# Experts of a two-layer trunk taken in an order that the chip decides, with weights addressed by loaded ids

## The chip, the cores and the metric

One core of one Trainium2 chip runs the whole program. The metric is device time in microseconds for one execution; lower is better. Engines are called PE (matmul), PEld (weight load of PE), DVE, ACT, POOL and SP, as in the profile. All weight transfers are issued by SP.

## What is computed

The input is 256 frames of 1024 float32 values. There are two layers. Each has a norm, an input projection with three token mixers, an output projection, and a second norm. Then layer 0 has a dense SwiGLU, and layer 1 the part that this change touches, the top-2-of-8 expert SwiGLU:

```
logits = t @ router                      # 256 tokens, 8 experts
top_v, top_i = lax.top_k(logits, 2)
gates = one_hot(top_i) * softmax(top_v)
for e in range(8):
    out = out + gates[:, e:e+1] * (silu(t @ wg[e]) * (t @ wu[e])) @ wd[e]
```

Each expert has three matrices of 1024 x 3584 float32, so 3 x 1024 x 3584 x 4 bytes = 44.04 MB, and eight experts have 352.3 MB. Every expert's weights are read whole, however many of the 256 tokens chose it. On average 64 tokens choose an expert (256 x 2 / 8). A final norm follows.

## The kernel before

**The weight stream.** A `Stream` (L72 to L134) holds a list of pieces of at most 1 MB, in the order in which PE will need them: the weights of the layers, then expert 0, 1, ..., 7. `loads` (L104) issues a piece as soon as a slot of the ring is free, by `load` (L156), which makes one transfer on SP's queue for each part of a slot (L162). `done` (L129) is called when the matmuls of a unit are through, and gives its slot back. There are 14 slots of 1 MB. `Room.take` (L783) adds four more, each of two halves of 0.5 MB, once the layers' working buffers are free. These 18 slots are all that the transfers can run ahead of PE.

**An expert.** Each expert is worked through in 7 chunks (NEC) of 512 columns. A chunk has 4.19 MB for the gate and up products and 2.10 MB for the down product, 6.29 MB in all. `experts` (L804) runs over e and c: the gate and up products of chunk c (`up_first`, L863), then `swish`, then the down product of the chunk before (`down`, L910), then three transposes that turn the new activations (`turn`, L891, the PE instructions of L894). With c = 1 the result of the expert before is put back into the rows of x (`combine`, L939). From c = 2 on, the tokens of the next expert are gathered, a step per chunk (`gather`, L823).

**Two sizes of expert.** The first 64 tokens of an expert go through matmuls of 64 columns (`wide`, L848, instructions of L852). If an expert has more than 64, up to 32 further tokens go through extra matmuls of 32 columns (`slim`, L855, instructions of L860), which read the same weights again. `count` (L758) sums the chosen tokens and makes the flag `many` per expert; `reach` (L811) loads it into a register of PE and `extra` (L815) branches on it. A third case (over 96 tokens, L1116 on) repeats the experts, and this input does not reach it. In the text that follows, an expert with the extra matmuls is called heavy, one without light.

**Expert 0's opening.** `opening` (L1074) works the gate product of expert 0's first chunk for all 256 tokens, and between its matmuls runs the router (`choose`, `places`, `counted`). Then `room.take()`, then the rest of `gather(0)`, then the loop. `weighing` (L1108) makes the gates in steps that lie behind the chunks of expert 0.

The order of the work on every engine is the order of the program (`manual_schedule`, L150): an instruction that waits holds up all that stands behind it on its engine.

Of the kernel before, what the change touches and what calls it, by code (L numbers as in the profile page):

```python
# [10 lines left out]
F32 = mybir.dt.float32  # L11
F32R = mybir.dt.float32r
I32 = mybir.dt.int32
AF = mybir.ActivationFunctionType
ALU = mybir.AluOpType
AX = mybir.AxisListType

P = 128
D = 1024
S = 256  # L20
NT = 2
# [10 lines left out]
E = 8  # L32
DFE = 3584
NEC = DFE // 512
EPS = 1e-6
QW = 1024
# [5 lines left out]
RAW = 2048  # L42
NRAW = 14
HALF = 64
# [27 lines left out]
class Stream:  # L72


    def __init__(self, load, split, chunks, slots):


        self.load, self.split = load, split
        self.pieces, self.units = [], []
        for ap, sizes, *more in chunks:  # L80
            whole = more[0] if more else False
            per = more[1] if len(more) > 1 else max(1, RAW // max(sizes))
            at = 0
            for j in range(0, len(sizes), per):
                group = sizes[j:j + per]
                off = 0
                for n in group:
                    self.units.append((len(self.pieces), off, n, off + n == sum(group), whole))
                    off += n
                b, at0 = (ap, at) if len(ap.shape) == 2 else (ap[at // RAW], at % RAW)  # L90
                self.pieces.append(b[:, at0:at0 + off])
                at += off
        self.tiles, self.parts, self.slots = {}, {}, deque(slots)
        self.loaded = self.cut = self.used = self.freed = 0
# [9 lines left out]
    def loads(self, upto=None):  # L104
        while self.slots and self.loaded < min(len(self.pieces) if upto is None else upto, len(self.pieces)):
            self.tiles[self.loaded] = self.slots.popleft()
            self.load(self.tiles[self.loaded], self.pieces[self.loaded])
            self.loaded += 1

    def release(self, i):  # L110
# [27 lines left out]
def trunk_kernel(ctx, tc, x_in, w_in, w_out, ffn_gu, ffn_d, moe_gu, moe_d, router,  # L138
                 params, gains, gm_gain, gm_wsT, pool_w, conv_pw, consts, pool_m, out):
    nc = tc.nc  # L140
# [10 lines left out]
    V, A, G, T = nc.vector, nc.scalar, nc.gpsimd, nc.tensor  # L151
# [31 lines left out]
    for l in range(DEPTH):  # L183
        col = 0
        for _, width in GROUPS:
            n = QW // width * width
# [5 lines left out]
        if l == 0:  # L192
            for c in range(NFC + 1):
                if c < NFC:
                    chunks.append((ffn_gu[c], [QW] * 4))
                if c:
                    chunks.append((ffn_d[c - 1], [QW] * 2))

    def expert_chunks(opening):
        ch = []  # L200
        last = E * NEC
        for i in range(last + 1):
            per = 1 if i >= last - 1 else 2
            if i < last:
                ch.append((moe_gu[i // NEC, i % NEC], *(([QW] * 8, True, per) if i or not opening else ([RAW] * 4, gates, 1))))
            if i:
                ch.append((moe_d[(i - 1) // NEC, (i - 1) % NEC], [QW] * 3 + [512] * 2 if i == last else [QW] * 4,
                           True, per))
        return ch

# [7 lines left out]
    iota1 = cst[:, CC_IOTA:CC_IOTA + P]  # L218
# [15 lines left out]
    gate = con.tile([P, NT, E], F32, name="gate")  # L234
    pos = con.tile([P, NT, E], F32, name="pos")
# [475 lines left out]
    lt = cst[:, CC_LT:CC_LT + E * E].rearrange("p (a b) -> p a b", a=E)  # L711
# [34 lines left out]
    def weigh_a(t, L, sv, vs):  # L746
        V.tensor_tensor(out=sv[:], in0=sel[:, t, :], in1=L[:], op=ALU.mult)
        V.tensor_reduce(out=vs[:], in_=sv[:], axis=AX.X, op=ALU.add)
        V.tensor_scalar(out=vs[:], in0=vs[:], scalar1=-0.5, scalar2=None, op0=ALU.mult)

    def weigh_b(t, L, sv, vs):
        A.activation(sv[:], L[:], AF.Tanh, bias=vs[:])

    def weigh_c(t, sv):
        V.tensor_scalar(out=sv[:], in0=sv[:], scalar1=0.5, scalar2=0.5, op0=ALU.mult, op1=ALU.add)
        V.tensor_tensor(out=gate[:, t, :], in0=sv[:], in1=sel[:, t, :], op=ALU.mult)

    def count(mo):  # L758

        ps = acc.tile([P, 512], F32, tag="acc", name="ps_n")  # L760
        for t in range(NT):
            T.matmul(ps[:, :E], ones, sel[:, t, :], start=(t == 0), stop=(t == NT - 1))
        many = mo.tile([P, E], I32, name="many")
        V.tensor_scalar(out=many[:], in0=ps[:, :E], scalar1=HALF + 0.5, scalar2=None, op0=ALU.is_gt)
        most = mo.tile([P, 1], F32, name="most")
        V.tensor_reduce(out=most[:], in_=ps[:, :E], axis=AX.X, op=ALU.max)
        mosti = mo.tile([P, 1], I32, name="mosti")
        V.tensor_copy(mosti[:], most[:])
        return many, mosti


    class Room:


        def __init__(self, mo):
            self.Sg = [mo.tile([P, NT, P], F32, name="Sg%d" % i) for i in range(2)]
            self.ST = [mo.tile([P, NT, P], F32R, name="ST%d" % i) for i in range(2)]
            self.s = mo.tile([P, 3, P], F32, name="silu2")
            self.ah = [mo.tile([P, 3, P], F32, name="eah%d" % i) for i in range(2)]
            self.yl = mo.tile([P, 512], F32R, name="yl")  # L780
            self.ys = None
# [22 lines left out]
    def experts(room, tok, W, gf, weighing=(), opening=None, counts=None):  # L804
# [3 lines left out]
        weighing = list(weighing)  # L808
# [6 lines left out]
        def extra(e, do):  # L815

            if counts:
                with tc.If(index[e] > 0):  # L818
                    do()
            else:  # L820
                do()
# [26 lines left out]
        def wide(ps, at, left, right, start, stop):  # L848

            for r in range(2):  # L850
                w = right(r)
                T.matmul(ps[HALF * r:HALF * (r + 1), at:at + w.shape[-1]], left, w,  # L852
                         start=start, stop=stop, skip_group_check=True)
# [25 lines left out]
        def flat(s):  # L879
            return s[:, :2, :].rearrange("p a b -> p (a b)")  # L880
# [71 lines left out]
        held, opened = opening(coming) if opening else (None, None)  # L952
        room.take()
        list(coming)
        pend, late = None, 0
        for e in range(E):
            coming = gather(e + 1) if e + 1 < E else iter(())
            for c in range(NEC):
                have = opened and e + c == 0
                if have:  # L960
                    us = held
                    for t in range(NT):
                        wide(room.gu, 0, room.Sg[0][:, t, FIRST], lambda r: opened[t][:, 256 * r:256 * (r + 1)],
                             t == 0, False)
                    for t in range(NT):
                        slim(room.gx, 0, room.Sg[0][:, t, LAST], lambda r: opened[t][:, P * r:P * (r + 1)],
                             t == 0, False)
                    up_first(e, us, True)
                    up_last(e, us, True)
                    A.activation(flat(room.s), room.gu[:, :256], AF.Copy)  # L970
                    A.activation(room.s[:, 2, :], room.gx[:, :P], AF.Copy)
                else:
                    W.pump(12)
                    us = [W.get() for _ in range(KD)]
                    up_first(e, us)
                    extra(e, lambda: up_last(e, us))
                for _ in range(4 if have else KD):
                    W.done()
                if c == 1:
                    if e == 0:  # L980
                        turn(room.ah[0])
                    else:
                        for hf in range(2):
                            combine(e - 1, hf, *late[hf])
                swish(have)
                if pend:
                    us = [W.get() for _ in range(4)]
                    down(*pend, us)
                    for _ in range(4):
                        W.done()  # L990
                    if pend[1] == NEC - 1:
                        late = [cut_y(hf) for hf in range(2)]
                    turn(room.ah[c % 2])
                if c > 1:
                    next(coming, None)
                if e == 0 and 1 < c < 2 + len(weighing):
                    weighing[c - 2]()
                pend = (e, c, room.ah[c % 2])
        e, c, ah = pend
        W.pump(5)  # L1000
# [45 lines left out]
    products, ps = mixing(0, mx, hh, hl, lambda: put(1, hs1))  # L1046
# [3 lines left out]
    with tc.tile_pool(name="ff", bufs=2) as ff:  # L1050
        g = gain(1)
        products, ps = ffn(ff, hh, hl, lambda: put(1, hs1), g)
# [9 lines left out]
    products, ps = mixing(1, mx, hh, hl, lambda: put(1, hs1))  # L1062
    mix_ctx.__exit__(None, None, None)
    mo = ctx.enter_context(tc.tile_pool(name="mo", bufs=1))
# [4 lines left out]
    Ls, counts = [None] * NT, []  # L1069
# [37 lines left out]

    def weighing():  # L1108
        sv = [(mo.tile([P, E], F32, name="sv%d" % t), mo.tile([P, 1], F32, name="vs%d" % t)) for t in range(NT)]
        return [lambda: [weigh_a(t, Ls[t], *sv[t]) for t in range(NT)],  # L1110
                lambda: [weigh_b(t, Ls[t], *sv[t]) for t in range(NT)],
                lambda: [weigh_c(t, sv[t][0]) for t in range(NT)]]

    room = Room(mo)
    experts(room, tok, W, gf, weighing(), opening, counts)
# [100 lines left out]
```

## Time and profile before

| | |
|---|---|
| median of 3 runs | 1272.27 us (1272.19 to 1273.04) |
| profiled execution | 1270.93 us |
| its span, first to last instruction | 1269.1 us |
| PE busy | 1176.0 us, 93% |
| DVE busy | 368.3 us, 29% |
| read from memory | 416.92 MB, 329 GB/s over the span |

The span is what the trace shows; the profiled execution's own time is 1.8 us longer, and the median of the runs is 1.3 us above that. A busy share of 93% for PE is an average over stages; the rate of the transfers, slice by slice, shows where PE waits for weights and where the transfers wait for room.

### The profile page before, as it was taken

What the parts mean: (1) busy time and instruction counts of PE and PEld (TensorE: products, weight loads), DVE (VectorE), ACT (ScalarE), POOL (GpSimd) and SP (SyncE); (2) the same over time, 40 slices, a digit from 0 to 9 for tenths busy, and PEclk for the clock granted to TensorE, in tenths of its full rate; (3) what the DMA queues carried; (4) which work ended last, traced back from release to release, by engine and by line L of the source; (5) the groups of instructions that cost most, each with busy time, mean ns of one, the idle gap of its engine ahead of it and who ended that gap; (6) DMA issues with size and microseconds to landing.
All of it is one profiled execution on the core that took longest, in us unless ns stands there. A gap on an engine that the chain in (4) does not pass through costs nothing. (4 is left out here: it accounts for less than half of the span.)

```text
span 1269.1 us, 17754 instructions
## 1 busy us (share of the span) xinstructions
PE 1176.0 (93%) x7278; PEld 611.7 (48%) x7278; DVE 368.3 (29%) x727; ACT 264.7 (21%) x555; POOL 78.9 (6%) x77
## 2 busy tenths in 40 slices
PE   6999999999999999999999999999999988888882
PEld 5867888889776333343334343433333322322220
DVE  5966455557962111100200020002112111002003
ACT  4545444445541001000100010001001010001001
POOL 2720000003700000000000000000000000000000
PEclk9999999999999999999999999999999999999996
DMA  9945555455346999999989899899999999999991
GB/s 369 425 158 183 196 171 196 136 196 204 125 149 237 418 424 423 423 426 404 370 356 364 350 373 340 335 382 404 424 423 424 424 423 423 424 425 423 422 401 50
DMA packets 72762, 419.72 MB, mean 331 GB/s; under 512 B 8768, under 2 KB 9280, under 8 KB 33856
## 3 DMA queue, kind: packets, MB, share of 16 engines
q1 hardware_dynamic: 72496, 417.77, 82.5%
q8 instruction: 88, 1.44, 0.4%
q10 hardware_dynamic: 144, 0.23, 0.1%
q14 instruction: 34, 0.28, 0.1%
HBM read 416.92 MB, written 1.05 MB: 329 GB/s over the span
## 5 line engine op out<-in xcount | busy, mean ns | idle before, releaser
L852 PE MATMUL ps_gu<-wraw,hh 128*64 128x512 f32 (+1 forms) x1504 | 338.0, 594 | 16.5 <-DMA wraw<-in_moe_gu_dram 15.8
L852 PEld LDWEIGHTS ps_gu<-wraw,hh 128*64 128x64 f32 x1504 | 102.4, 137 | 222.9 <-issue 170.4
L852 PE MATMUL ps_y<-wraw,eah 128*64 128x512 f32 x592 | 137.4, 599 | 11.4 <-DMA wraw<-in_moe_wd_dram 5.1
L167 ACT ACTIVATE whi<-wraw 128x1024 fp32r<-128x1024 f32 (+1 forms) x106 | 108.2, 1027 | 113.9 <-PE ps_gu L245 65.4
L168 DVE TENSOR_TENSOR wlo<-wraw,whi 128x1024 fp32r<-128x1024 f32 (+1 forms) x83 | 101.1, 1218 | 93.6 <-ACT whi L167 93.2
L886 DVE TENSOR_TENSOR silu<-silu,ps_gu 128x256 f32<-128x256 f32 x56 | 23.5, 419 | 339.3 <-ACT silu L885 334.1
L885 ACT ACTIVATE silu<-ps_gu 128x256 f32<-128x256 f32 x55 | 21.1, 384 | 364.2 <-PE ps_gu L852 364.2
L896 DVE COPY eah<-ps_tp 128x256 f32<-128x256 f32 x56 | 23.8, 424 | 226.5 <-ACT eah L895 226.3
L852 PEld LDWEIGHTS ps_y<-wraw,eah 128*64 128x64 f32 x592 | 41.3, 136 | 98.6 <-issue 72.7
L243 PE MATMUL ps_gu<-whi,hh 128*128 128x512 f32 x192 | 77.6, 404 | 1.1 <-ACT hh L239 0.8
L244 PE MATMUL ps_gu<-wlo,hh 128*128 128x512 f32 x192 | 76.1, 396 | 0.8 <-DVE wlo L168 0.8
L245 PE MATMUL ps_gu<-whi,hl 128*128 128x512 f32 x192 | 76.1, 396 | 0.0
L256 POOL TENSOR_TENSOR ss<-ss,mh 128x1 f32<-128x1 f32 x10 | 5.5, 551 | 1117.9 <-DVE ss L255 1117.9
L852 PE MATMUL ps_y<-wmore,eah 128*64 128x512 f32 x304 | 70.2, 599 | 3.0 <-PEq L818 2.5
L895 ACT ACTIVATE eah<-ps_tp 128x128 f32<-128x128 f32 x56 | 15.5, 278 | 255.9 <-PE ps_tp L894 255.7
L852 PE MATMUL ps_gu<-wmore,hh 128*64 128x512 f32 x288 | 66.9, 600 | 1.3 <-DMA wmore<-in_moe_gu_dram 1.0
L860 PE MATMUL ps_gx<-wraw,hh 128*32 128x256 f32 (+1 forms) x1184 | 66.6, 374 | 0.0
L390 DVE SCALAR_TENSOR_TENSOR ps_conv<-cb,par,ps_conv 128x256 f32<-128x256 f32 x150 | 62.7, 481 | 0.9
L860 PEld LDWEIGHTS ps_gx<-wraw,hh 128*32 128x32 f32 x1184 | 36.6, 110 | 33.4 <-issue 11.7
L168 POOL TENSOR_TENSOR wlo<-wraw,whi 128x768 fp32r<-128x768 f32 (+1 forms) x23 | 48.9, 2138 | 50.3 <-ACT whi L167 36.1
L852 PEld LDWEIGHTS ps_y<-wmore,eah 128*64 128x64 f32 x304 | 21.4, 136 | 46.9 <-issue 40.1
L243 PEld LDWEIGHTS ps_gu<-whi,hh 128*128 128x128 f32 x192 | 36.1, 188 | 10.1 <-ACT hh L239 1.7
(205 smaller groups left out, 1294.8 us busy)
## 6 DMA issues: line engine op xcount, KB each, us to landing
wraw<-in_moe_gu_dram SPq DMA_DIRECT2D x184, 1024.0 KB, 12.7
wraw<-in_moe_wd_dram SPq DMA_DIRECT2D x72, 1024.0 KB, 14.1
wmore<-in_moe_wd_dram SPq DMA_DIRECT2D x76, 512.0 KB, 14.7
wmore<-in_moe_gu_dram SPq DMA_DIRECT2D x72, 512.0 KB, 10.3
wraw<-in_ffn_gu_dram SPq DMA_DIRECT2D x22, 1024.0 KB, 4.9
wraw<-in_ffn_d_dram SPq DMA_DIRECT2D x11, 1024.0 KB, 4.9
wraw<-in_w_out_dram SPq DMA_DIRECT2D x8, 1024.0 KB, 7.2
wraw<-in_w_in_dram SPq DMA_DIRECT2D x6, 1024.0 KB, 4.9
```

What stands on the lines that cost most here:

```text
L167: A.activation(hi[:, :n], src, AF.Copy)
L168: (G if pool else V).tensor_tensor(out=lo[:, :n], in0=src, in1=hi[:, :n], op=ALU.subtract)
L243: T.matmul(ps, xh, wh, start=start, stop=False)
L244: T.matmul(ps, xh, wl, start=False, stop=False)
L245: T.matmul(ps, xl, wh, start=False, stop=stop)
L390: V.scalar_tensor_tensor(out=o, in0=i, scalar=wcol, in1=part[:] if k == n else sums[c], op0=ALU.mult, op1=ALU.add)
L852: T.matmul(ps[HALF * r:HALF * (r + 1), at:at + w.shape[-1]], left, w, start=start, stop=stop, skip_group_check=True)
L860: T.matmul(ps[QUARTER * r:QUARTER * (r + 1), at:at + n], left, w, start=start, stop=stop, skip_group_check=True)
L885: A.activation(flat(s), room.gu[:, :256], AF.Silu)
L886: V.tensor_tensor(out=flat(s), in0=flat(s), in1=room.gu[:, 256:], op=ALU.mult)
L895: A.activation(ah[:, :1, :], tp[:, :1, :], AF.Copy)
L896: V.tensor_copy(ah[:, 1:, :], tp[:, 1:3, :])
```

## The change

After the counts are known, DVE ranks experts 1 to 7 by their count. The positions 1 to 7 of the loop then take the experts in the order heaviest, lightest, second heaviest, second lightest, and so on. Expert 0 stays first. `arrange` builds a 7 x 7 matrix that says which expert goes to which position, and with `permute` brings the counts, the flags, the places of the tokens (`pos`) and later the gates into the new order. The expert's number for each position is loaded into a register of SP (`nc.sync.value_load`, seven of them), and the piece of weights is addressed by that register when its transfer is issued (`bass.ds(ids[p], 1)`). Nothing else of an expert's work changes.

```diff
@@ Stream.__init__
+                if callable(ap):
+                    self.pieces.append(lambda ap=ap, at=at, off=off: ap(at // RAW, at % RAW, off))
+                else:
+                    b, at0 = (ap, at) if len(ap.shape) == 2 else (ap[at // RAW], at % RAW)
+                    self.pieces.append(b[:, at0:at0 + off])
@@ Stream.loads
-            self.load(self.tiles[self.loaded], self.pieces[self.loaded])
+            piece = self.pieces[self.loaded]
+            self.load(self.tiles[self.loaded], piece() if callable(piece) else piece)
@@ expert_chunks
+    ids = {}
+    def of(w, p, c):
+        if p == 0:
+            return w[0, c]
+        return lambda i, at, n: w[bass.ds(ids[p], 1), c, i][:, :, at:at + n].rearrange("a p n -> p (a n)")
...
-                ch.append((moe_gu[i // NEC, i % NEC], *(([QW] * 8, True, per) ...
+                ch.append((of(moe_gu, i // NEC, i % NEC), *(([QW] * 8, True, per) ...
-                ch.append((moe_d[(i - 1) // NEC, (i - 1) % NEC], ...
+                ch.append((of(moe_d, (i - 1) // NEC, (i - 1) % NEC), ...
@@ count
-        V.tensor_scalar(out=many[:], in0=ps[:, :E], scalar1=HALF + 0.5, scalar2=None, op0=ALU.is_gt)
+        n = mo.tile([P, E], F32, name="counts")
+        V.tensor_copy(n[:], ps[:, :E])
+        V.tensor_scalar(out=many[:, :1], in0=n[:, :1], scalar1=HALF + 0.5, scalar2=None, op0=ALU.is_gt)
@@ new
+    def permute(tab, turns):
+        by, tmp = turns
+        V.tensor_tensor(out=tmp[:], in0=by[:], in1=tab.unsqueeze(1).broadcast_to([P, E - 1, E - 1]), op=ALU.mult)
+        V.tensor_reduce(out=tab, in_=tmp[:], axis=AX.X, op=ALU.add)
+    def arrange(mo, many, n):
+        m = E - 1
+        La = n[:, 1:].unsqueeze(2).broadcast_to([P, m, m])
+        Lb = n[:, 1:].unsqueeze(1).broadcast_to([P, m, m])
+        ...
+        V.tensor_tensor(out=tmp[:], in0=Lb, in1=La, op=ALU.is_equal)
+        V.tensor_tensor(out=by[:], in0=Lb, in1=La, op=ALU.is_gt)
+        V.tensor_tensor(out=tmp[:], in0=tmp[:], in1=lt[:, 1:, 1:], op=ALU.mult)
+        V.tensor_tensor(out=by[:], in0=by[:], in1=tmp[:], op=ALU.add)
+        ...
+        V.tensor_reduce(out=rank, in_=by[:], axis=AX.X, op=ALU.add)
+        V.tensor_scalar(out=up, in0=rank, scalar1=2.0, scalar2=1.0, op0=ALU.mult, op1=ALU.add)
+        V.tensor_scalar(out=down, in0=rank, scalar1=-2.0, scalar2=float(2 * m), op0=ALU.mult, op1=ALU.add)
+        V.tensor_tensor(out=up, in0=up, in1=down, op=ALU.min)
+        V.tensor_tensor(out=by[:], in0=iota1[:, :m]..., in1=up..., op=ALU.is_equal)
+        turns = by, tmp
+        V.tensor_copy(rank, iota1[:, :m])
+        permute(rank, turns)
+        V.tensor_copy(idi[:], rank)
+        permute(n[:, 1:], turns)
+        V.tensor_scalar(out=many[:, 1:], in0=n[:, 1:], scalar1=HALF + 0.5, scalar2=None, op0=ALU.is_gt)
+        for t in range(NT):
+            permute(pos[:, t, 1:], turns)
+        for p in range(1, E):
+            ids[p] = nc.sync.value_load(idi[0:1, p - 1:p], min_val=1, max_val=m)
+        return turns
@@ experts
         room.take()
         list(coming)
+        turns = arrange(room.mo, *counts[::2]) if opening else None
@@ weighing: a fourth step, behind chunk 5 of expert 0
+                lambda turns: [permute(gate[:, t, 1:], turns) for t in range(NT)]]
```

## Rows read from the trace of the kernel before

**Rows 1.** Page, part 2: PE's clock, transfer rate, 40 slices of 31.7 us.

```profile
PEclk9999999999999999999999999999999999999996
GB/s 369 425 158 183 196 171 196 136 196 204 125 149 237 418 424 423 423 426 404 370 356 364 350 373 340 335 382 404 424 423 424 424 423 423 424 425 423 422 401 50
```

**Rows 2.** Windows, all engines: length, busy by engine, PE clock, DMA share, GB/s.

```profile
494.20:617.70 123.50, 122.27 (x1071) 50.61 (x1071) 15.30 (x35) 10.27 (x29) 0.00 (x0) 1.00 1.00 415
617.70:741.20 123.50, 122.29 (x1075) 50.59 (x1071) 14.72 (x34) 10.27 (x29) 0.00 (x0) 1.00 0.91 354
741.20:861.50 120.30, 118.79 (x1011) 48.83 (x1007) 14.62 (x34) 10.16 (x29) 0.00 (x0) 1.00 0.92 360
...
861.50:950.90 89.40, 84.95 (x404) 31.61 (x401) 13.94 (x34) 9.50 (x29) 0.00 (x0) 1.00 1.01 422
861.50:1028.20 166.70, 158.59 (x752) 59.23 (x748) 26.61 (x64) 18.18 (x55) 0.00 (x0) 1.00 1.01 422
...
950.90:1042.60 91.70, 85.51 (x400) 31.04 (x400) 13.85 (x35) 9.51 (x29) 0.00 (x0) 1.00 1.01 424
1042.60:1147.40 104.80, 89.30 (x400) 29.16 (x401) 14.17 (x35) 9.51 (x29) 0.00 (x0) 1.00 1.01 424
1147.40:1236.70 89.30, 76.48 (x314) 21.24 (x314) 11.74 (x27) 7.58 (x23) 0.00 (x0) 0.98 1.01 417
```

**Rows 3.** Windows of L860 alone, the extra matmuls: PE and PEld busy.

```profile
494.20:617.70 123.50, 39.09 (x672) 20.40 (x672) 1.00 1.00 415
...
741.20:861.50 120.30, 35.50 (x612) 18.43 (x608) 1.00 0.92 360
...
861.50:950.90 89.40, 0.09 (x4) 0.00 (x0) 1.00 1.01 422
```

**Rows 4.** Waits of SP's queue, 618 to 861 us: total, times, longest.

```profile
SPq L162 <- PE ps_gx L860: 125.7, 49, 11.0
```

**Rows 5.** Waits of SP's queue, 1028 to 1237 us.

```profile
SPq L162 <- DMA wraw<-in_moe_gu_dram: 94.9, 50, 2.9
```

**Rows 6.** Timeline of DVE around the opening: start, duration, instruction, idle before.

```profile
386.97 0.22 DVE L732 TENSOR_TENSOR gt<-gt,eq 128x64 f32<-128x64 f32 x1
387.23 0.22 DVE L734 TENSOR_REDUCE rank<-gt 128x8 f32<-128x64 f32 x1
...
392.74 0.47 DVE L827 TENSOR_SCALAR Sg<-cst,pos 128x128 f32<-128x128 f32 x2
...
397.40 0.42 DVE L839 COPY hh<-ps_tp 128x256 f32<-128x256 f32 x1 [1.30 <-ACT hh L838]
403.02 0.42 DVE L886 TENSOR_TENSOR silu<-silu,ps_gu 128x256 f32<-128x256 f32 x1 [5.20 <-ACT silu L970]
```

**Rows 7.** Timeline of PE in the same stretch.

```profile
393.07 3.87 PE L836 MATMUL ps_tp<-Sg,tok 128*128 128x128 f32 x32 [0.71 <-DVE Sg L827]
...
411.61 0.52 PE L894 MATMUL ps_tp<-cst,silu 128*128 128x128 f32 x3 [0.16 <-PEq L818]
```

**Rows 8.** Timeline of SP's queue in the same stretch: weight transfers issued.

```profile
403.19 0.80 SPq L162 DMA_DIRECT2D wraw<-in_moe_gu_dram  x2
...
411.59 1.75 SPq L162 DMA_DIRECT2D wraw<-in_moe_gu_dram  x4
```

**Rows 9.** Line L1116, a register loaded from a tile: duration ns min/median/max.

```profile
L1116 SPq TENSOR_LOAD <-mosti x1: 750/750/750, 1259.7 to 1259.7; - x1
L1116 SPq FUSED_REGOPS  x1: 191/191/191, 1260.5 to 1260.5; - x1
```

**Rows 10.** Line L162, issues of expert weights on SP: duration ns min/median/max.

```profile
L162 SPq DMA_DIRECT2D wraw<-in_moe_gu_dram x192: 327/328/1543, 278.2 to 1220.7; - x192
L162 SPq DMA_DIRECT2D wraw<-in_moe_wd_dram x77: 327/328/1532, 330.4 to 1231.8; - x77
L162 SPq DMA_DIRECT2D wmore<-in_moe_wd_dram x76: 327/328/1169, 387.2 to 1228.1; - x76
L162 SPq DMA_DIRECT2D wmore<-in_moe_gu_dram x72: 327/328/692, 390.2 to 1200.4; - x72
```

More of the change, by code (lines that the diff above doesn't have):

```diff
@@ L89, in __init__ @@
                     off += n
-                b, at0 = (ap, at) if len(ap.shape) == 2 else (ap[at // RAW], at % RAW)
-                self.pieces.append(b[:, at0:at0 + off])
+                if callable(ap):
[3 more added lines that the diff above has]
+                    self.pieces.append(b[:, at0:at0 + off])
                 at += off
@@ L204, in expert_chunks @@
             if i < last:
-                ch.append((moe_gu[i // NEC, i % NEC], *(([QW] * 8, True, per) if i or not opening else ([RAW] * 4, gates, 1))))
+                ch.append((of(moe_gu, i // NEC, i % NEC), *(([QW] * 8, True, per) if i or not opening else ([RAW] * 4, gates, 1))))
             if i:
-                ch.append((moe_d[(i - 1) // NEC, (i - 1) % NEC], [QW] * 3 + [512] * 2 if i == last else [QW] * 4,
+                ch.append((of(moe_d, (i - 1) // NEC, (i - 1) % NEC), [QW] * 3 + [512] * 2 if i == last else [QW] * 4,
                            True, per))
@@ L768, in count @@
         V.tensor_copy(mosti[:], most[:])
-        return many, mosti
+        return many, mosti, n
+    def permute(tab, turns):
[6 more added lines that the diff above has]
+        Lb = n[:, 1:].unsqueeze(1).broadcast_to([P, m, m])
+        by = mo.tile([P, m, m], F32, name="by")
+        tmp = mo.tile([P, m, m], F32, name="by2")
+        V.tensor_tensor(out=tmp[:], in0=Lb, in1=La, op=ALU.is_equal)
+        V.tensor_tensor(out=by[:], in0=Lb, in1=La, op=ALU.is_gt)
+        V.tensor_tensor(out=tmp[:], in0=tmp[:], in1=lt[:, 1:, 1:], op=ALU.mult)
+        V.tensor_tensor(out=by[:], in0=by[:], in1=tmp[:], op=ALU.add)
+        turn = mo.tile([P, 3, m], F32, name="turn")
+        rank, up, down = (turn[:, i, :] for i in range(3))
+        V.tensor_reduce(out=rank, in_=by[:], axis=AX.X, op=ALU.add)
+        V.tensor_scalar(out=up, in0=rank, scalar1=2.0, scalar2=1.0, op0=ALU.mult, op1=ALU.add)
+        V.tensor_scalar(out=down, in0=rank, scalar1=-2.0, scalar2=float(2 * m), op0=ALU.mult, op1=ALU.add)
+        V.tensor_tensor(out=up, in0=up, in1=down, op=ALU.min)
+        V.tensor_tensor(out=by[:], in0=iota1[:, :m].unsqueeze(2).broadcast_to([P, m, m]),
+                        in1=up.unsqueeze(1).broadcast_to([P, m, m]), op=ALU.is_equal)
+        turns = by, tmp
+        V.tensor_copy(rank, iota1[:, :m])
+        permute(rank, turns)
+        idi = mo.tile([P, m], I32, name="idi")
+        V.tensor_copy(idi[:], rank)
[6 more added lines that the diff above has]
+        return turns
     class Room:
         def __init__(self, mo):
+            self.mo = mo
             self.Sg = [mo.tile([P, NT, P], F32, name="Sg%d" % i) for i in range(2)]
@@ L996, in experts @@
                 if e == 0 and 1 < c < 2 + len(weighing):
-                    weighing[c - 2]()
+                    weighing[c - 2](turns)
                 pend = (e, c, room.ah[c % 2])
@@ L1109, in weighing @@
         sv = [(mo.tile([P, E], F32, name="sv%d" % t), mo.tile([P, 1], F32, name="vs%d" % t)) for t in range(NT)]
-        return [lambda: [weigh_a(t, Ls[t], *sv[t]) for t in range(NT)],
-                lambda: [weigh_b(t, Ls[t], *sv[t]) for t in range(NT)],
-                lambda: [weigh_c(t, sv[t][0]) for t in range(NT)]]
+        return [lambda turns: [weigh_a(t, Ls[t], *sv[t]) for t in range(NT)],
+                lambda turns: [weigh_b(t, Ls[t], *sv[t]) for t in range(NT)],
+                lambda turns: [weigh_c(t, sv[t][0]) for t in range(NT)],
+                lambda turns: [permute(gate[:, t, 1:], turns) for t in range(NT)]]
     room = Room(mo)
```

## The prediction

> **What bounds the kernel now.** I read the forty slices first. After slice 13 the transfers run at about 424 GB/s, then fall to 335 to 404 for ten slices, then return to 424 to the end [rows 1]. PE's clock is full throughout, so the dip is not the clock's. Second, windows cut at the L894 transposes of each expert's first chunk: the seven experts after expert 0, the last one up to the transposes of its last chunk [rows 2]. Third, the same windows for the extra matmuls alone [rows 3]. The three stretches with extra matmuls (the second reads like the first) are those of experts 1, 2 and 3; after 861 us there are none. So experts 1, 2, 3 are heavy and 0, 4, 5, 6, 7 light.
>
> A heavy expert takes 123.5 us and PE is busy for 122.3 of them: PE is the bound. SP's queue waits there for PE's matmuls to give slots back [rows 4]: the ring is full and the transfers idle, at 354 and 360 GB/s. A light expert takes PE 89.4 us where the ring still has stock, which is so up to 1028.2 [rows 2]; the next take longer, up to 104.8 us. That is the transfers' own pace: 44.04 MB at 424 GB/s are 103.9 us. SP waits there for earlier transfers to land [rows 5]. So three slow experts in a row fill the ring and leave the transfers idle, and four quick ones in a row then empty it and leave PE idle.
>
> How much does the ring hold? What PE still has to read, less what still arrives, is the stock. After 494.2 us 296.6 MB arrive (51.3, 43.7, 43.3, 37.7, 38.9, 44.4 and 37.2, each row's length times its rate). PE has then used eight gate-and-up and seven down parts, 48.2 of 352.3 MB, and needs 304.1: the stock is 7.5 MB. By the same sum it is 13.7 MB at 861.5, after the heavy experts: full (172.0 needed, 158.3 still to come). At 1042.6 it is 2.2 MB: empty (83.9 and 81.7). A full ring therefore carries 11.5 MB of surplus.
>
> **The change, part by part.**
>
> The order. Ranks by count put the three heavy experts at ranks 0, 1, 2 of seven, and the positions from 1 on take ranks 0, 6, 1, 5, 2, 4, 3. With expert 0 the run of experts is light, heavy, light, heavy, light, heavy, light, light. PE's work is the same. If it never waits for weights, the time from 494.2 us to the last expert's transposes is the three heavy stretches as they are (367.3 us), two light ones of 89.4, and the 166.7 of the 13 chunks after a full ring [rows 2]: 712.8 us. Now it is 742.5 (the sum of the seven windows). The difference is 29.7 us.
>
> Does PE never wait? One heavy expert brings 123.5 x 0.424 = 52.4 MB and uses 44.04: +8.3. One light expert brings 37.9: -6.1. From 7.5 the first heavy one fills the ring to 13.7; a light one leaves 7.6, far above 2.2; the next heavy one fills it again. After the third heavy one the ring is full and two light ones end the run: that is the stretch 861.5 to 1028.2 over again, which PE went through in 166.7 us at its own pace, and after it only the last down part is left. From the transfers' side: 296.6 MB at 424 GB/s take 699.5 us; with a full ring the first heavy expert loses as now, 123.5 x 9/424 = 2.6 us, and the two others 2.2 MB or 5 us each. That is 712.2, against PE's 712.8. The two bounds meet within a microsecond, so little is left to gain beyond this, and any loss on the transfers' side soon shows.
>
> A figure of the Trainium skill speaks against it. The transfers ran at 422 to 424 GB/s over 375 us and more [rows 2]. The Trainium skill's page "DMA: Bandwidth & Descriptors", section Specifications, gives a limit of memory per core of about 358 GB/s. By that figure 44.04 MB would need an estimated 123 us, a heavy expert's time, and the order would be worth nothing; the trace disagrees wherever the ring has room.
>
> `arrange` on DVE: 20 small operations on 7 x 7 or fewer elements. Dependent operations on 64 elements start 0.26 us apart [rows 6], so 20 x 0.26 = 5.2 us. They begin when the last copy of `gather(0)` ends, 397.8 us, and DVE then has nothing to do until 403.0. Its result of 403.0 is wanted by the transposes of 411.6 [rows 7]. So the cost is nothing; without that cover the whole 5.2 us would stand on PE's path.
>
> The extra copy of the counts stands ahead of the selection matrix `Sg` (392.7), and PE waited 0.71 us for that [rows 6, 7]. It adds one dependent step: +0.3 us. The wait for the flags by PE's register loads comes chunks later. The gates' fourth step has two operations for each half of the tokens, under a microsecond or so on DVE, which idles most of each chunk: nothing.
>
> The seven register loads stand in SP's queue and wait for the ids, the 13th operation of `arrange`: 397.8 + 13 x 0.26 = 401.2 us. Behind them stand all further transfers. One load took SP 0.75 us with 0.19 of arithmetic behind it [rows 9]. Seven in a row are 6.6 us, to 407.8, where the next issue stood at 403.2 [rows 8]. From below it is nothing, if loads overlap; from above 4.6 us of idle transfers, or 2.0 MB. I take the upper value. It comes out of the stock: 7.5 becomes 5.5 MB at 494.2, still above empty, and the first heavy expert makes up 8.3. So it costs PE nothing. It would begin to cost at 5.3 MB, 12 us of hold-up.
>
> Each transfer of experts 1 to 7 gets its address from a register. No row shows such an issue. From below: as now, 0.33 us [rows 10]. From above: the whole sequence of a register load each time, 0.33 + 0.94 = 1.27 us. There are 417 issues for 352.3 MB [rows 10], so 351 after 494.2 us, one in 2.0 us. At either end SP keeps up (446 us of 713), and the transfers in flight cover it. I take a value near the lower end, since the arithmetic of one register took 0.19 us [rows 9], and put its cost at nothing.
>
> Sum against the profiled execution: 1270.9 - 29.7 + 0.3 = 1241.5 us. The median of the runs stands 1.3 us above that execution: 1242.8 us.
>
> **Rivals.**
>
> Slower transfers. If transfers addressed by register move less per second (fewer in flight, or a pause at each), the transfers' side becomes the bound. At 410 GB/s 296.6 MB take 723.4 us, the ring is never full, and the time is 1242.8 + 10.6 = 1253 us. At 400 it is 741.5 and the gain is gone. For it: the bounds meet within a microsecond. Against it: sizes, rows and queue stay the same. Chance 0.11.
>
> SP becomes the bound, the rival on the slower side. Each issue would have to take over 742.5 / 351 = 2.1 us, by address arithmetic, a check of bounds, or a drain at each. At 2.3 us the stretch takes 807 us and the kernel 1337. For it: the operation is in no row, and everything of the stream stands behind it in one queue. Against it: the upper bound from rows is 1.27. Chance 0.08.
>
> No change. Either the order on the chip isn't the one that I read (heavy experts still side by side), or the low rate of the heavy stretches is memory's limit and not a full ring: 354 to 360 GB/s [rows 2] is also what 44.04 MB in 123.5 us come to, 357. Then the transfers would not fill the ring in a heavy expert between light ones. Against the second: SP waits for PE there. About 1272 us. Chance 0.07, of which the memory limit has 0.02.
>
> **How the numbers follow.** The forecast has 0.74, with a range of its own of 1238 to 1248: PE may wait a little in the last two experts, where a full ring just lasts (1 MB less of it is 2.4 us), or wait less in the tail. The whole range is 1237 to 1256; it takes in most of the slower transfers and leaves out SP as the bound and no change. A difference of 0.2% (2.5 us) is about what a measurement of this kernel can tell from none. Faster by more: 0.74 + 0.11 = 0.85. The no-change case gives 0.07 within 0.2%, and SP as the bound 0.08 slower.
>
> **What would show it.** Right: the extra matmuls of L860 come in three stretches of some 120 us with a light expert of some 90 us after each; the rate stays over 410 GB/s but for a short dip at the end of each heavy expert; no window of a light expert takes over 93 us before the last two; SP's waits for the extra matmuls shrink from 126 us in two heavy experts [rows 4] to some 10 us in all three. DVE's block ends before the product of L886 is wanted at 411.6. Wrong: light experts of 100 us or more with 424 GB/s or less and SP waiting on landings (slower transfers), SP's issues of L162 at over 2 us each (SP as the bound), or the flags and extra matmuls side by side as before.

## The result, and the profile after

The changed kernel takes 1239.8 us (median of 4 runs, 1238.7 to 1240.7) against 1272.7 us: a ratio of 0.974, interval 0.9724 to 0.9755. The forecast was 1242.8 us in a range of 1237 to 1256. The profiled execution took 1240.74 us, its span 1239.0.

The page after, part 2, as in [rows 1]:

```profile
PEclk9999999999999999999999999999999999999995
GB/s 367 425 182 187 170 189 184 148 158 216 189 154 136 374 419 423 427 423 423 416 406 423 424 425 422 417 389 421 424 425 424 423 390 394 423 425 423 422 400 41
```

The ten slices at 335 to 404 GB/s are gone. Three short dips are left, to 406, 389 and 390. The windows after, cut at the same points as [rows 2]: the transposes of each expert's first chunk (now L948), then those of the last chunk, then the end. Columns as there.

```profile
494.00:614.30 120.30, 118.75 (x1007) 48.94 (x1007) 15.24 (x35) 10.15 (x29) 0.00 (x0) 1.00 1.01 422
614.30:706.60 92.30, 88.47 (x468) 33.30 (x464) 13.72 (x34) 9.61 (x29) 0.00 (x0) 1.00 1.01 418
706.60:826.90 120.30, 118.79 (x1008) 48.94 (x1008) 15.18 (x35) 10.15 (x29) 0.00 (x0) 1.00 1.00 413
826.90:919.30 92.40, 88.41 (x467) 33.38 (x465) 13.87 (x34) 9.60 (x29) 0.00 (x0) 1.00 1.01 423
919.30:1039.50 120.20, 118.69 (x1007) 48.85 (x1006) 15.02 (x35) 10.14 (x29) 0.00 (x0) 1.00 1.00 409
1039.50:1128.80 89.30, 85.08 (x404) 31.59 (x401) 13.64 (x34) 9.50 (x29) 0.00 (x0) 1.00 1.01 421
1128.80:1205.50 76.70, 71.58 (x314) 22.60 (x315) 11.73 (x27) 7.58 (x23) 0.00 (x0) 1.00 1.01 421
1205.50:1239.00 33.50, 9.94 (x35) 3.87 (x35) 11.03 (x20) 5.70 (x14) 1.09 (x2) 0.62 0.16 53
```

Heavy and light alternate, 120 and 92 us. The last two light experts no longer take 104.8 and 89.3 us, but 89.3 and 76.7. The seven windows sum to 711.5 us, where they were 742.5: 31 us less. The stretch behind them took 1.1 us more (33.5 for 32.4), and the profiled executions are 30.2 us apart. No heavy expert stands any longer at 354 GB/s.

The chip's decision, on DVE (start, duration, idle before) and then on SP (line L821, duration ns min/median/max):

```profile
397.54 0.20 DVE L799 TENSOR_TENSOR by<-counts 128x49 f32<-128x49 f32 x1
...
401.15 0.20 DVE L790 TENSOR_REDUCE pos<-by 128x7 f32<-128x49 f32 x1
402.82 0.42 DVE L940 TENSOR_TENSOR silu<-silu,ps_gu 128x256 f32<-128x256 f32 x1 [1.46 <-ACT silu L1025]
```

```profile
L821 SPq TENSOR_LOAD <-idi x7: 263/269/470, 400.2 to 403.9; - x7
L821 SPq FUSED_REGOPS  x7: 147/147/183, 400.7 to 404.2; - x7
```

DVE's 20 operations end at 401.4 and its next old work starts at 402.8 (403.0 before). SP's loads run from 400.2 to 404.4. The next weight transfers and PE's wait for `Sg` then stand at:

```profile
404.85 0.81 SPq L167 DMA_DIRECT2D wraw<-in_moe_gu_dram  x2
```

```profile
392.88 3.87 PE L890 MATMUL ps_tp<-Sg,tok 128*128 128x128 f32 x32 [0.90 <-DVE Sg L881]
```

So the transfers are 1.7 us later than in [rows 8], and PE waits 0.2 us longer than in [rows 7]. The issue of a transfer by register, line L167:

```profile
L167 SPq FUSED_REGOPS  x367: 43/46/56, 448.5 to 1199.7; - x184
L167 SPq DMA_DIRECT2D wraw<-in_moe_gu_dram x192: 327/333/548, 277.9 to 1189.4; - x192
L167 SPq MOVE wraw<-in_moe_gu_dram x168: 29/29/37, 449.4 to 1189.3; - x168
```

The address costs 0.046 + 0.029 us, and the issue itself 0.333 instead of 0.328 [rows 10].

### The profile page after: what moved, and what is told of

The parts are those of the page before. It is cut to its first block, busy times and chain, and to the rows that moved or that the text cites. A ratio compares the mean times of both kernels' runs of the same rounds, so it can differ in the third digit from the quotient of the medians.

```text
span 1239.0 us, 18535 instructions
## 1 busy us (share of the span) xinstructions
PE 1168.0 (94%) x7278; PEld 617.8 (50%) x7278; DVE 371.8 (30%) x752; ACT 264.5 (21%) x555; POOL 78.8 (6%) x77
## 5 line engine op out<-in xcount | busy, mean ns | idle before, releaser
L906 PE MATMUL ps_gu<-wraw,hh 128*64 128x512 f32 (+1 forms) x1504 | 331.9, 591 | 1.0 <-DMA wraw<-in_moe_gu_dram 1.0
L914 PEld LDWEIGHTS ps_gx<-wraw,hh 128*32 128x32 f32 x1184 | 36.8, 110 | 33.2 <-issue 11.7
```

What stands on the lines that cost most here:

```text
L914: T.matmul(ps[QUARTER * r:QUARTER * (r + 1), at:at + n], left, w, start=start, stop=stop, skip_group_check=True)
```

## The experiments

In each kernel the lines of the changed kernel are meant unless the diff says otherwise. First the base again. The kernel before ran beside every one of them, and each ratio is to those runs of it.

> The changed kernel again, as the base for the runs beside it on the same chip. Every theory: 1239.8 us, within 1.5 us of its first runs.

It took 1239.6 us (1237.8 to 1240.7, five runs); ratio to the kernel before 0.9745, interval 0.9732 to 0.9759.

**Is it the order, or something else of the change?** Everything of the change, but in the old order:

```diff
-        V.tensor_tensor(out=up, in0=up, in1=down, op=ALU.min)
+        V.tensor_copy(up, iota1[:, :m])
```

> Everything of the change (ranking, permutations, register loads, addresses from registers), but the permutation is set to the identity, so experts 1 to 7 run in their old order, three heavy ones side by side. Theory (the order alone makes the gain): the kernel before, 1272.6 us, plus 0 to 1 us. Rival (some other part of the change makes the gain): 1240 us. If registers slow the transfers: over 1274 us, since the last two experts run at the transfers' pace.

1270.2 us, ratio 0.9989 (0.998 to 0.9999). With the old order the gain is gone, though ranking, loads and register addresses are all there. The low rates of [rows 1] are back, and after them the transfers run at their full rate:

```profile
GB/s 368 425 160 183 193 173 199 136 195 202 130 149 202 423 420 422 423 427 419 375 360 367 338 383 332 358 370 402 425 423 423 426 423 423 425 423 423 423 413 64
```

From the transposes of expert 1's first chunk (494.5 us) to the last ones (1237.1) it takes 742.6 us, for 742.5 in the kernel before, and the last two experts run at the transfers' pace there too. So the registers don't slow the transfers, and the ranking costs nothing that shows. The 0.1% on the fast side lies, in the profiled executions, behind the last transposes (30.5 us for 32.4); its cause is open.

**What do deciding and addressing cost?** The same order written into the program:

```diff
-        return lambda i, at, n: w[bass.ds(ids[p], 1), c, i][:, :, at:at + n].rearrange("a p n -> p (a n)")
+        return w[(0, 2, 7, 1, 5, 3, 6, 4)[p], c]
...
-        for p in range(1, E):
-            ids[p] = nc.sync.value_load(idi[0:1, p - 1:p], min_val=1, max_val=m)
```

> The same order of experts (0, 2, 7, 1, 5, 3, 6, 4) written into the program: no register loads on SP, no address from a register; DVE's ranking and permutations stay. Theory (the order alone makes the gain, the deciding and the addressing are hidden): the same as the changed kernel within 1 us, and the idle stretch of the transfers near 400 us shorter by the 4.4 us of the loads. Rival (registers cost something on every one of 351 transfers, and the transfers' side is the bound): 2 us faster or more.

1240.7 us, ratio 0.9755 (0.9741 to 0.9768), 1.1 us above the base, which is within the spread, and not the 2 us below it that the rival asked for. Its first transfers in this stretch stand at 403.8 instead of 404.9 us, so only 1 us of hold-up went away and not 4.4: without any loads they stood at 403.2 [rows 8]. The loads and the addresses cost nothing that can be measured; DVE's part of the decision is still in this kernel, and for that the run above stands.

**Does the ring's stock explain which orders are good?** The ranking turned round, lightest first:

```diff
-        V.tensor_tensor(out=up, in0=up, in1=down, op=ALU.min)
+        V.tensor_scalar(out=up, in0=rank, scalar1=-1.0, scalar2=float(m), op0=ALU.mult, op1=ALU.add)
```

> The ranking turned round: lightest first, the three heavy ones last. Theory of the ring's stock: the four light ones empty the stock and run at the transfers' pace, 404 us from 494 us to the first heavy one's chunk; then two heavy ones of 123.5 us and six chunks of the last, 107 us: PE path 47 us longer than in the changed kernel, 1288 us, slower than before. Rival (any order that puts the heavy ones elsewhere gains, or it matters only that they don't stand at positions 1 to 3): 1240 to 1272 us.

1287.7 us, ratio 1.0122 (1.0106 to 1.0139). The windows: the four light experts and the first heavy one's first chunk, then two heavy experts, then six chunks of the last:

```profile
490.80:903.00 412.20, 357.90 (x1661) 119.42 (x1662) 57.07 (x137) 38.13 (x116) 0.00 (x0) 1.00 1.01 423
903.00:1150.40 247.40, 244.78 (x2142) 101.08 (x2141) 29.80 (x69) 20.54 (x58) 0.00 (x0) 1.00 0.99 404
1150.40:1252.50 102.10, 101.72 (x894) 40.21 (x890) 11.68 (x26) 8.24 (x23) 0.00 (x0) 1.00 0.67 246
```

In the first window the transfers run at 423 GB/s and PE is idle for 54 us; in the last PE is busy throughout and the transfers have nothing left to bring (246 GB/s). The same work, the same bytes, 48 us more: while the four light experts empty the ring PE waits, and the heavy ones after them cannot give that time back. The total was forecast within 1 us, but that is in part luck. The first stretch ended at 903.0 us where 898 was expected, and the last took 102.1 us where 107 was expected; the two misses cancel.

**Is it the ring's depth that carries it?** Without the four further slots, in both orders:

```diff
-                ring.extend(more)
-                W.slots.extend(more)
-                W.loads()
```

> The changed kernel without the four further slots: 14 slots instead of 18, 4.2 MB less. Theory: a full ring's surplus falls from 11.5 to 7.3 MB; one light expert between heavy ones takes 6.1 and still doesn't empty it, the last 13 chunks take 11.5 and do: 4.2 MB at 0.424 MB/us are 10 us, 1250 us. Rival (the ring's depth is not what carries the surplus): 1240 us; rival (each light expert already empties it): 1260 us or more.

> The kernel before without the four further slots. Theory: the ring is full through the three heavy experts as before, and its 4.2 MB less of surplus are used up sooner by the light ones: 10 us slower, 1282.5 us, so that the change's gain at 14 slots is as large as at 18. Rival (the gain of the change comes from depth that the old order doesn't use): unchanged 1272.6 us.

1247.9 us (0.9816, 0.98 to 0.9833) and 1280.9 us (1.0074, 1.0057 to 1.0091): 8.3 and 9.1 us slower, for 10 expected, and the gain is 33 us, where it is 32 with 18 slots. At 14 slots the light experts at positions 2 and 6 still run at PE's pace and only the last one waits:

```profile
614.40:706.60 92.20, 88.41 (x467) 33.21 (x463) 13.66 (x34) 9.61 (x29) 0.00 (x0) 1.00 1.01 424
1039.70:1128.80 89.10, 84.97 (x404) 31.50 (x400) 13.63 (x34) 9.50 (x29) 0.00 (x0) 1.00 1.01 425
1128.80:1212.90 84.10, 73.74 (x315) 21.66 (x316) 11.76 (x27) 7.58 (x23) 0.00 (x0) 1.00 1.01 423
```

**How much lost transfer time does it stand?** Further register loads behind the seven, which hold SP up (6, 14 and 35 of them):

```diff
+        for p in range(14):
+            nc.sync.value_load(idi[0:1, p % m:p % m + 1], min_val=1, max_val=m)
```

> The changed kernel with 14 further register loads on SP behind its seven, 0.58 us each: all transfers behind them are held up by 8.1 us more near 405 us. Theory (the stock of the ring covers it: 7.1 MB at 494 us less 3.4 is 3.7, above the empty 2.2, and the next heavy experts make it up): no change, 0 to 1 us. Rival (the transfers' side and PE's meet within a microsecond, so lost transfer time shows at the end): 8 us slower.

> The same with 35 further loads, 20.2 us of hold-up, 8.6 MB. Theory of the stock: 7.1 less 8.6 is 3.7 MB short of the empty ring's 2.2, so PE waits 8 to 9 us before or in the first heavy expert, and the rest is made up: 1248 us. Rival (lost transfer time shows at the end one for one): 1260 us. If the stock is larger than reckoned: 1240 us.

> The changed kernel with 6 further register loads on SP, 3.5 us of hold-up near 405 us. From the two larger doses (8.1 us cost 4.7, 20.2 us cost 15.4) a margin of 3 to 5 us is left before lost transfer time shows at the end: 0 to 1 us slower. If there is no margin at all (a loss in proportion): 2 to 3.5 us slower.

The first transfers came 3.5, 8.2 and 20.3 us later than the changed kernel's 404.85. The times: 1240.6 us (0.975, 0.9737 to 0.9763), 1244.3 (0.9781, 0.9766 to 0.9796) and 1255.0 (0.9866, 0.9851 to 0.9881), that is 1.0 (within the spread), 4.7 and 15.4 us over the base. The stock theory failed for the two larger ones, and so did loss one for one: some 3.5 to 5 us of lost transfers are free, the rest shows. Where the 8.2 us went, first in the base's windows at the end (the three chunks ahead of the last one, then the last of the weights), then in those of the kernel with 14 further loads:

```profile
1154.80:1190.90 36.10, 33.96 (x154) 11.16 (x155) 3.13 (x9) 2.49 (x9) 0.00 (x0) 1.00 1.02 422
...
1204.70:1206.70 2.00, 1.47 (x9) 0.65 (x9) 0.42 (x1) 0.28 (x1) 0.00 (x0) 1.00 0.79 315
1206.70:1208.70 2.00, 1.96 (x10) 0.43 (x6) 0.00 (x0) 0.00 (x0) 0.00 (x0) 1.00 0.29 110
```

```profile
494.40:614.60 120.20, 118.69 (x1007) 48.75 (x1007) 15.13 (x35) 10.15 (x29) 0.00 (x0) 1.00 1.02 424
614.60:706.90 92.30, 88.46 (x468) 33.29 (x464) 13.69 (x34) 9.61 (x29) 0.00 (x0) 1.00 1.01 424
706.90:827.20 120.30, 118.78 (x1008) 48.85 (x1008) 15.19 (x35) 10.15 (x29) 0.00 (x0) 1.00 1.02 423
827.20:919.60 92.40, 88.41 (x467) 33.36 (x464) 13.83 (x34) 9.61 (x29) 0.00 (x0) 1.00 1.01 419
919.60:1039.90 120.30, 118.74 (x1008) 48.79 (x1007) 15.04 (x35) 10.14 (x29) 0.00 (x0) 1.00 1.01 416
...
1155.20:1195.70 40.50, 35.26 (x154) 10.45 (x155) 3.13 (x9) 2.49 (x9) 0.00 (x0) 1.00 1.01 416
...
1207.50:1209.50 2.00, 1.85 (x8) 0.21 (x6) 0.00 (x0) 0.00 (x0) 0.00 (x0) 1.00 0.64 259
1209.50:1211.50 2.00, 1.47 (x9) 0.66 (x9) 0.42 (x1) 0.28 (x1) 0.00 (x0) 1.00 0.38 147
1211.50:1213.50 2.00, 1.96 (x10) 0.42 (x6) 0.00 (x0) 0.00 (x0) 0.00 (x0) 1.00 0.11 43
```

Up to 1040 us PE is no later than in the base but for 0.4 us: the stock did cover the hold there. The same three chunks near the end then take 40.5 us for 36.1, with the same 154 matmuls. Taking 424 GB/s as full rate, the five windows lose 3.7 us; the changed kernel's own five lose 9.5 (0.6, 1.3, 3.1, 0.2 and 4.3). So by this sum 5.8 of the 8.2 us were made up. And in the last 6 us of the stream the rate falls in steps while the last transfers land: that loses 3.9 us against 2.0 in the base. 8.2 - 5.8 + 1.9 = 4.3, of 4.7 measured. The longest hold shows both parts. PE waits already in expert 0, whose next expert starts 8.6 us late (502.5 for 493.9), as the stock said. It is 8.6 us late still when the last expert's first chunk is through (1137.3 for 1128.8); then it waits again, and the three chunks near the end take 43.4 us for 36.1.

**What is left on the transfers' side?** The flags at zero, so that experts 1 to 7 have no extra matmuls:

```diff
-        V.tensor_scalar(out=many[:, :1], in0=n[:, :1], scalar1=HALF + 0.5, scalar2=None, op0=ALU.is_gt)
+        V.tensor_scalar(out=many[:, :1], in0=n[:, :1], scalar1=1000.0, scalar2=None, op0=ALU.is_gt)
...
-        V.tensor_scalar(out=many[:, 1:], in0=n[:, 1:], scalar1=HALF + 0.5, scalar2=None, op0=ALU.is_gt)
+        V.tensor_scalar(out=many[:, 1:], in0=n[:, 1:], scalar1=1000.0, scalar2=None, op0=ALU.is_gt)
```

> The changed kernel with every flag zero: the extra matmuls are left out, so tokens beyond the 64th of an expert are missing from the output. PE's work from 494 us falls by some 100 us. Theory (the transfers' side is a bound close behind PE's): the transfers run without a pause, 297 MB from 494 us at 0.4215 MB/us end at 1199 us, engines apart by 2 to 4 us, and the end follows 29 us after the last landing: 1230 to 1233 us, only 7 to 10 us below the changed kernel. Rival (PE is the one bound, transfers have room): below 1200 us.

1235.3 us, ratio 0.9711 (0.9696 to 0.9725). PE is busy for 609 us from 494 to 1202 us, some 80 us less than in the changed kernel up to its last transposes (690), and the time falls by 4.3 us. That is far from the rival's 1200, but 7 to 10 us had been expected, and the time is 2 us above the expected range. SP waits mostly for landings, as in [rows 5]. No slice dips as in the kernel before, but the rate is not quite flat. Between 800 and 1100 us it was 421 GB/s, where 424 had been seen; why is open:

```profile
GB/s 366 425 188 186 172 181 194 145 162 209 188 164 136 351 419 423 426 423 423 426 423 424 425 424 423 425 420 423 422 420 421 418 418 420 422 426 413 422 376 42
```

```profile
SPq L167 <- DMA wraw<-in_moe_gu_dram: 303.3, 160, 3.2
```

The changed kernel thus stands close to both bounds at once: PE's path, and some 4 us below it the transfers' stream as it runs without a pause. An order alone could hardly gain more than those 4 us; other orders that alternate heavy and light were not run.

## Why the prediction was right, point by point

- **The reading of before.** A full ring in three heavy experts, an empty one in the last light ones: the old order with all the new code, the reversed order and the 14 slots bear it out. The reversed order's time was worked out by this reading alone (1288 and 1287.7), though two misses of 5 us cancelled in it.
- **The order.** PE's path without a wait was put at 712.8 us and took 711.5. The parts were further off than the sum: the three heavy stretches took 6.5 us less than before and the two light ones 5.9 us more than the 89.4 each, since 68 extra matmuls of a heavy expert (3.7 us) fall into the window of the light one that follows. Nor did PE go wholly without a wait. The last chunk but one took 13.3 us (1178.1 to 1191.4), where the two before it took 11.7, and part of what PE waited for there were landings.
- **The transfers' side.** 712.2 was reckoned, with 12.6 us lost to a full ring. The first five windows show 9.5. The stream that never paused gained only 4.3 us, so the two bounds lie some 4 us apart and not within one. The rivals of slower transfers and of SP as the bound fell: an address from a register costs 0.08 us, near the lower end as chosen, where 2.1 would have been needed.
- **Memory's limit.** That the heavy stretches' 354 to 360 GB/s were memory's own limit (the Trainium skill, "DMA: Bandwidth & Descriptors", section Specifications, has about 358) fell too: the second and third heavy experts now run at 413 and 409 GB/s, and at 423 and 416 after the hold of 8.2 us. One core ran here; what two cores reading at once would get, no run shows. The prediction puts 422 to 424 GB/s at 375 us and more; [rows 2] have it for 286 us, and 417 in the last 89.
- **`arrange`.** 5.2 us reckoned, 3.8 measured (397.5 to 401.4), hidden either way. Its operations started every 0.19 us on average, since only some depend on the one before.
- **The copy of the counts.** 0.3 us reckoned, 0.2 measured.
- **The register loads.** The upper bound was taken, 0.94 us each and 4.6 us of hold-up. The first took 0.84, the others 0.58, and the hold-up was 1.7 (1.0 against the order written into the program). It fell into the free 3.5 to 5 us.
- **What failed: the price of a longer hold.** "It would begin to cost at 5.3 MB, 12 us of hold-up" is wrong: 8.2 us cost 4.7. I had looked at PE's stock at the start only, where it holds, and had taken the later heavy experts' refilling as free. The same section had said that the two bounds meet and that any loss on the transfers' side soon shows. That sentence was the right one.
- **A sign that was wrong.** SP's waits for the extra matmuls were to fall from 126 us to some 10. They still sum to 81 us over the three heavy experts (waits of SP's queue, 494 to 1040 us):

```profile
SPq L167 <- PE ps_gx L914: 80.8, 45, 10.8
```

  The transfers ran at 409 to 422 GB/s meanwhile: SP waits for a slot while earlier transfers are still moving. A wait in the issuing queue does not show that the transfers idle; that has to be read from their rate.
- **Execution and median.** I added 1.3 us from the profiled execution to the median, as before. After, the profiled execution is 1.0 us above the median. That is 2.3 of the 3.0 us between forecast and result; the sum against the profiled execution was 1241.5, and it took 1240.7. That this lies so near is in part luck: the windows gained 1.3 us more than forecast, and the stretch behind them, which the sum left as it was, took 1.1 us more.

## What to carry to other kernels

When stages alternate between two bounds and a buffer lies between them, the order of the stages is a cost: put a stage that fills the buffer ahead of each that drains it, and no more in a row than the buffer holds. Work out both bounds for the new order to the end, since where one ends the other takes over: here a gain of 31 us was to be had and some 4 beyond it. A decision made on the chip from data can cost nothing, if its operations fall where their engine idles and the addresses go through registers of the issuing queue.

## What the runs showed of the hardware

A register load on SP took 0.26 to 0.47 us, less than the single one of [rows 9] with 0.75. An address from a register costs 0.08 us per transfer, and the rate is the same as without: in the old order with register addresses 423 to 426 GB/s from the last heavy expert to the last two slices, 422 to 425 in the kernel before.

When the last transfers have all been issued, the rate falls in steps, 259, 147 and 43 GB/s, over 6 us after a hold and over 4 us without one. The busy share of the sixteen transfer engines falls with it (0.64, 0.38 and 0.11), so fewer of them are busy, and those move data at nearly the full pace. That reads as some of them being through before others; the share is a mean over all sixteen, and which ones is not shown. Why the end was drawn out further after a hold was not tried.
